# Attention weights turned through DRAM instead of by sixteen on-chip copies a head

## The chip, the cores and the metric

The kernel runs on one core of a Trainium2 chip. Its five engines (PE or TensorE, DVE or VectorE, ACT or ScalarE, POOL or GpSimd, SP or SyncE) have a queue each and run side by side; DMA engines move data between DRAM and SBUF. The metric is the device time of one execution in microseconds, the median of several runs.

## What is computed

One layer of an encoder: an RMS norm, one input projection, attention with eight query heads over two key/value heads and 512 tokens, a linear recurrence in both directions (LRU) over 1024 channels, a norm of each group by itself, gates, and one output projection.

```python
def hybrid_layer(x, ...):
    h = rms_norm(x, norm_w)
    proj = jnp.einsum('bsd,de->bse', h, w_in)          # 512 x 2048 by 2048 x 4608
    q, k, v, g_attn, xr, g_lru = jnp.split(proj, SPLITS, axis=-1)
    attn_out = attention_group(q, k, v, q_norm_w, k_norm_w)
    lru_out = lru_group(xr, conv_w, conv_b, lru_wa, lru_ba, lru_wx, lru_bx, lru_lambda)
    mixed = jnp.concatenate([rms_norm(attn_out, attn_norm_w) * jax.nn.silu(g_attn),
                             rms_norm(lru_out, lru_norm_w) * jax.nn.silu(g_lru)], axis=-1)
    return x + jnp.einsum('bse,ed->bsd', mixed, w_out)

def block(qb):                                         # in attention_group
    s = jnp.einsum('bkgqd,bksd->bkgqs', qb, k_t) * scale
    p = jax.nn.softmax(s, axis=-1)
    return jnp.einsum('bkgqs,bksd->bkgqd', p, v_t)
```

All is float32. Each product is made of three TensorE products of values split in a high and a low part (`mm3`: high by high, high by low, low by high).

## The kernel before

The work is one long program whose TensorE order is written out by hand. Generators are woven: `weave(fill, chain)` runs `chain`, and for each number n that it yields takes n steps of `fill`. The `fill` during attention is `gates()`, the projections for the gates: three groups of 512 columns (LRU gate in two halves, first half of the attention gate), each of 32 fill steps. A fill step is six matmuls of 128x128 by 128x512; four fill steps use up one chunk of `w_in`, 256 rows by 512 columns (512 KB). A chunk is loaded by SyncE (`wraw`, line 205) into a ring of three tiles, split by ACT (`wh`, line 216) and DVE (`wl`, line 217); during attention there are four pairs `wh`, `wl`, so room for two chunks. `take()` fetches the chunk two ahead of the one that it hands out.

`attention()` (line 644) is the `chain`. It first yields `BEGIN` = 8 fill steps, then goes through 32 steps, four (t = 0 to 3, one block of 128 queries each) for each of the eight heads, and six more for what lags. In a step `weights` makes one block of the attention weights: scores (`mm3` into a PSUM bank), row maximum (DVE), exponential (ACT, with the row sum), reciprocal (DVE), scaling (POOL, line 599) and a DVE transpose of 32x32 blocks into the tile `u` (line 600). `u` holds a head: on partition 32i + r, four sections a of 512 elements (2 KB). For the product with `v` the blocks must still change places between partitions: section a of partition group i has to go to partition group a, place i.

That is what `moved` does (line 605). Before, SyncE issues sixteen copies from SBUF to SBUF for each head, 32 partitions by 2 KB each (line 610): eight right after the head's last block, eight in the next step. Then ACT and DVE split the result `pt`, of which there is one buffer, into `ph` and `pl` (lines 620, 621). `values` (line 624), the product with `v`, comes `LATE` = 2 steps after the last block of the next head, that is six steps after the head's own last block: head h's `values` stand in step 4h + 9. It also adds the squares for the group norm (`asum`, line 642). Every step then yields `STEPS` = 2 fill steps.

During attention SyncE's order is written out too (`manual_schedule`): its DMAs leave in the order in which the program states them, and one that must wait holds all behind it. On SyncE are the loads of `w_in`, the copies for `moved`, and in steps 8 to 15 eight copies from DRAM to DRAM (`copy_to`, line 768). POOL issues 24 accumulating DMAs of 256 KB (`add_to`, line 771), one in each of steps 0 to 7 and 16 to 31, each behind the scaling of that step; their results are read only by the output product.

After attention twelve fill steps are left. Before, six of them are run, then the group statistics (`group_rstd`, line 685, eight small matmuls over `asum`), four more, `rows` (line 274, which spreads the result over the partitions), and the last two. Ahead of them in the program stand the builds of the four LRU pairs for the output product (`build`, `seven`: DVE and ACT). Then the fourth gate group (32 fill steps) is woven with `later()`, which normalizes two pairs of heads, yields 6, and gates them; then follows the output product (`outputs`, line 895 on TensorE).

Of the kernel before, what the change touches and what calls it, by code (L numbers as in the profile page):

```python
# [11 lines left out]
F32 = mybir.dt.float32  # L12
F32R = mybir.dt.float32r
# [4 lines left out]
P = 128  # L18
# [3 lines left out]
NT = SEQ // P  # L22
HD = 128
NH = 8
# [18 lines left out]
WARM, WARM2 = 14, 5  # L43


BEGIN, STEPS, LATE = 8, 2, 2


H = 256
# [2 lines left out]
B = 32  # L52
NQ = P // B
# [9 lines left out]
def hybrid_kernel(  # L63
# [20 lines left out]
    nc = tc.nc  # L84
# [28 lines left out]
    dram = ctx.enter_context(tc.tile_pool(name="dram", bufs=1, space=bass.MemoryType.DRAM))  # L113
# [3 lines left out]
    def nm(s):  # L117
        cnt[0] += 1
        return f"{s}_{cnt[0]}"
# [10 lines left out]
    def at(tag, bufs, shape, dt=F32):  # L130
        return pools["att"].tile([P, *shape], dt, tag=tag, bufs=bufs, name=nm(tag))
# [10 lines left out]
    def mm():  # L142
        return ps.tile([P, SEQ], F32, tag="mm", name=nm("mm"))

    def const(shape, name, dt=F32):
        return cp.tile(list(shape), dt, tag=name, name=name)

    def f(ap):
        return ap.bitcast(F32)
# [116 lines left out]
    def rsqrt_mean(dst, src, n, width):  # L266

        nc.gpsimd.tensor_scalar(dst, src, 1.0 / n, EPS, op0=ALU.mult, op1=ALU.add)
        nc.gpsimd.tensor_tensor(dst, dst, nhalf[:, :width], op=ALU.pow)
# [4 lines left out]
    def rows(dst, col, dg):  # L274

        shape = [P, NT, P]
        part = [const([P, NT], nm("part")) for _ in range(2)]
        parts = [dg() for _ in part]
        nc.vector.tensor_copy(part[0].bitcast(F32R), col)
        nc.vector.tensor_sub(part[1], col, part[0])  # L280
        for c, d in zip(part, parts):
            nc.vector.tensor_mul(
                d, ident[:, None, :].broadcast_to(shape), c[:, :, None].broadcast_to(shape)
            )
        pb = mm()
        for k, d in enumerate(parts):
            d = d.rearrange("p t q -> p (t q)")
            nc.tensor.matmul(pb, ones_r, d, start=k == 0, stop=k == 1)
        nc.vector.tensor_copy(dst, pb)
# [59 lines left out]
    def drain(fill):  # L349
        for _ in fill:  # L350
            pass
# [30 lines left out]
    sums = {}  # L382
# [197 lines left out]
    def turned(rot, h):  # L580

        q = at("q", 2, (2, SEQ), F32R)
        split_ps(turn(rot, h), q[:, 0, :], q[:, 1, :])
        return q[:, 0, :], q[:, 1, :]
# [3 lines left out]
    def weights(q, g, t, turned_):  # L588

        qh, ql = q  # L590
        tt = slice(t * P, (t + 1) * P)
        sc = mm()
        mm3(sc, qh[:, tt], ql[:, tt], kth[g], ktl[g], True, True)
        mx, sm = (at(n, 6, (1,)) for n in ("mx", "sm"))
        nc.vector.tensor_reduce(mx, sc, axis=AX.X, op=ALU.max, negate=True)  # L595
        p = at("p", 3, (SEQ,))
        nc.scalar.activation(p, sc, AF.Exp, bias=mx, accum_out=sm)  # L597
        nc.vector.reciprocal(sm, sm)  # L598
        last_scale[0] = nc.gpsimd.tensor_scalar(p, p, sm, 0.0, op0=ALU.mult, op1=ALU.add).ins  # L599
        nc.vector.transpose(  # L600
            turned_[:, :, :, t, :].rearrange("p a s c -> p s a c"),
            p.rearrange("p (s a c) -> p s a c", a=NQ, c=B),
        )

    def moved(turned_):

        pt = at("pt", 1, (NQ, NT, P))
        for i in range(NQ):
            for a in range(NQ):
                nc.sync.dma_start(  # L610
                    pt[a * B : (a + 1) * B, i].rearrange("p s x -> p (s x)"),
                    turned_[i * B : (i + 1) * B, a].rearrange("p s t c -> p (s t c)"),
                )
            if i % 2:
                yield
        hi, lo = at("ph", 1, (NT, SEQ), F32R), at("pl", 1, (NT, SEQ), F32R)
        hi4, lo4 = (v.rearrange("p s (i x) -> p i s x", i=NQ) for v in (hi, lo))
        for s in range(0, NT, 2):
            ss = slice(s, s + 2)
            nc.scalar.copy(hi4[:, :, ss], pt[:, :, ss])  # L620
            nc.vector.tensor_sub(lo4[:, :, ss], pt[:, :, ss], f(hi4[:, :, ss]))
        yield hi, lo

    def values(h, hi, lo):

        gs = slice(h // G * HD, (h // G + 1) * HD)
        o = mm()
        for s in range(NT):
            mm3(o, vh[s][:, gs], vl[s][:, gs], hi[:, s], lo[:, s], s == 0, s == NT - 1)
        if h % 2 == 0:  # L630
            ap_[h // 2] = aring.tile([P, 2, SEQ], F32, name=nm("av"))
        av, asum = ap_[h // 2][:, h % 2, :], sums["a"]
        nc.vector.tensor_copy(
            av.rearrange("p (t i c) -> p i t c", i=NQ, c=B),
            o.rearrange("p (i t c) -> p i t c", i=NQ, c=B),
        )
        if h == 0:
            nc.scalar.activation(asum, av, AF.Square)
        else:
            sq = at("p", 3, (SEQ,))  # L640
            nc.scalar.activation(sq, av, AF.Square)
            nc.gpsimd.tensor_add(asum, asum, sq)

    def attention(rots, transfers):

        qs, pts = {h: turned(rots[0], h) for h in range(1)}, {}
        yield BEGIN
        last = NH * NT
        for i in range(last + NT + LATE):
            h, t = divmod(i, NT)  # L650
            if i < last:
                if t == 0:
                    u = at("u", 2, (NQ, NT, NT, B))
                weights(qs[h], h // G, t, u)
                next(transfers, None)
                if t == 0 and h + 1 < NH:
                    qs[h + 1] = turned(rots[(h + 1) // G], (h + 1) % G)
                if t == NT - 1:
                    pts[h] = moved(u)
                    next(pts[h])  # L660
            if t == 0 and 0 < h <= NH:
                next(pts[h - 1])
                pts[h - 1] = next(pts[h - 1])
            h, t = divmod(i - LATE, NT)
            if t == NT - 1 and h > 0:
                values(h - 1, *pts.pop(h - 1))
            yield STEPS


    def gate(gs, pairs, row, sig):  # L670
# [11 lines left out]
    def fin_s(shape=(P, SEQ), dt=F32):  # L682
        return pools["fin"].tile(list(shape), dt, tag="s", bufs=2, name=nm("s"))

    def group_rstd(src, name, n):

        pr = mm()
        for t in range(NT):
            nc.tensor.matmul(
                pr[:, t : t + 1], src[:, t * P : (t + 1) * P], ones[:, 0:1], start=True, stop=True  # L690
            )
        r = const([P, NT], name)
        nc.vector.tensor_copy(r, pr[:, :NT])
        rsqrt_mean(r, r, n, NT)
        return r

    gbc = const([P, SEQ], "gbc")

    def normed(pair):
        nc.vector.tensor_mul(pair, pair, gbc[:, None, :].broadcast_to([P, 2, SEQ]))  # L700
# [27 lines left out]
    def kept(pool, i):  # L728
        return [
            pools[pool].tile([P, 7, H], F32R, tag=f"{t}{i}", bufs=1, name=nm(t))  # L730
            for t in ("mh", "ml")
        ]
# [302 lines left out]
    for step in proj_feat(C_XR, a1, first, given):  # L1035
# [8 lines left out]
        c, e = step  # L1044
# [17 lines left out]
    fill = proj_feat(C_XR + SEQ, a2)  # L1062
    wsums = first_sums()

    def with_sums(fill, n, first=0):

        for k, _ in enumerate(fill):
            if k >= first and (k - first) % n == 0:
                next(wsums, None)
            yield  # L1070

    fill = with_sums(fill, 8, 16)
# [23 lines left out]
    def both():  # L1096
        yield from q_proj(C_Q, a4)
        yield from q_proj(C_Q + SEQ, a5)

    fill = with_sums(both(), 5)  # L1100
# [40 lines left out]
    fill = gates()  # L1141
    with tc.manual_schedule(engines={mybir.EngineType.SP}):
        weave(fill, attention(rots, last_sums()))
# [14 lines left out]
    def build(i, pair, parts):  # L1158
        mixed[i][1] = parts
        seven(pair, *parts)  # L1160

    for q in range(4):
        build(q, hp[q], kept("fin", q))
    for _ in range(6):
        next(fill)
    with tc.high_priority():
        r = group_rstd(sums["a"], "r_a", NH * HD)
    for _ in range(4):
        next(fill)
    with tc.high_priority():  # L1170
        rows(gbc, r, lambda: fin_s((P, NT, P), F32R))
    drain(fill)


    def later():
        for pair in ap_[:2]:
            normed(pair)
        yield 6
        todo = gate(late, ap_[:2], R_AN, fin_s)
        for _ in range(3):  # L1180
            yield next(todo)
        build(4, ap_[0], [hring.tile([P, 7, H], F32R, name=nm(t)) for t in ("mh", "ml")])
        yield from todo
        for pair in ap_[2:]:
            normed(pair)

    acc = []
    fill = proj_feat(C_GA + SEQ, acc, take=take)
# [26 lines left out]
    last = ExitStack()  # L1215
# [47 lines left out]
```

## Time and profile before

| | us |
|---|---|
| median of three runs | 682.94 |
| the runs | 681.77 to 684.16 |
| the profiled execution | 681.03 |
| its span, first to last instruction | 679.3 |

The mean clock granted to TensorE over the span is 0.977 of full speed. In the page an engine's busy time counts its instructions without branches, semaphores and DMA issues; matmuls are pipelined, so PE's busy time isn't time at its peak. "PEld" is the loading of the stationary operand, "SPq" and the like an engine's queue, "DMA a<-b" a transfer from b to a. The chain that ended last is followed back from the last instruction, at each step to what released it. L610 is line 610 of the kernel. The lines themselves stand in the prediction, where they are used.

### The profile page before, as it was taken

The page shows a single profiled execution, that of the slowest core. Times are in us where ns is not written, and L with a number is a line of the kernel's source. Part 1 is how long each engine was busy: PE and PEld are TensorE (multiplying, and loading weights), DVE is VectorE, ACT ScalarE, POOL GpSimd, SP SyncE. Part 2 cuts the span into 40 slices and gives each one's busy share as a digit, 9 for nine tenths or more (in the row PEclk, how much of TensorE's full clock was granted, in tenths as well). Part 3 has the DMA queues.
Part 4 walks back from the last instruction along what each step waited for, and adds up shares of the span by engine and source line. Part 5 has one row for each costly group of instructions (what it writes and reads, how often), then busy time and mean ns, then how long its engine had stood idle before and what let it go on. Part 6 is the DMA issues. An engine that isn't in the chain of part 4 may idle for free.

```text
span 679.3 us, 8373 instructions
## 1 busy us (share of the span) xinstructions
PE 646.6 (95%) x2835; PEld 527.8 (78%) x2835; DVE 485.6 (71%) x788; ACT 346.2 (51%) x586; POOL 102.1 (15%) x137
## 2 busy tenths in 40 slices
PE   9999999999999998979879888799999999999997
PEld 7888888888888886867657766588888888888885
DVE  5888699958788638555855558438946777797775
ACT  3535997599468225433734337325524554444441
POOL 0001000100034003331113423202000000110010
PEclk9999999999999999998879989799999999999999
DMA  8854676666565312385366756752335675797252
GB/s 282 279 155 126 142 207 150 167 163 171 157 224 178 116 40 62 49 195 147 99 171 145 152 121 146 179 180 62 94 124 186 184 238 194 262 340 265 94 190 93
DMA packets 62459, 110.85 MB, mean 163 GB/s; under 512 B 6744, under 2 KB 17104, under 8 KB 62416
## 3 DMA queue, kind: packets, MB, share of 16 engines
q1 hardware_dynamic: 54384, 92.48, 42.0%
q0 software_dynamic: 7712, 17.31, 14.8%
q10 hardware_dynamic: 320, 0.53, 0.3%
q8 instruction: 22, 0.36, 0.2%
q14 instruction: 21, 0.17, 0.1%
HBM read 97.71 MB, written 25.17 MB: 181 GB/s over the span
## 4 chain that ended last, share of the span: by engine, by line
PE 79%; SPq 7%; DMA 5%; DVE 3%; ACT 3%; issue 2%; POOL 0%; DVEq 0%; ACTq 0%; POOLq 0%
PE pj L152 16%; PE pj L154 16%; PE pj L153 16%; PE mm L895 13%; PE pj L895 10%; SPq L610 6%; DMA wr<-in_w_in_dram 4%; PE mm L154 2%; PE mm L152 2%; PE mm L153 2%; DVE wl L217 1%; PE mm L242 1%; ACT wh L216 1%; PE pj L308 1%; DMA pt<-u 1%
## 5 line engine op out<-in xcount | busy, mean ns | idle before, releaser
L152 PE MATMUL pj<-x,wh 128*128 128x512 f32 x376 | 152.9, 407 | 20.6 <-ACT wh L216 20.6
L154 PE MATMUL pj<-x,wl 128*128 128x512 f32 x376 | 150.9, 401 | 2.9 <-DVE wl L217 2.9
L153 PE MATMUL pj<-x,wh 128*128 128x512 f32 x376 | 150.8, 401 | 0.0
L216 ACT CAST wh<-wr 128x512 fp32r<-128x512 f32 x143 | 83.9, 618 | 82.8 <-PE pj L154 26.1
L217 DVE TENSOR_TENSOR wl<-wr,wh 128x512 fp32r<-128x512 f32 x144 | 95.2, 694 | 33.5 <-ACT wh L216 25.3
L152 PEld LDWEIGHTS pj<-x,wh 128*128 128x128 f32 x376 | 73.1, 195 | 37.4 <-ACT wh L216 22.6
L747 ACT CAST wh<-wr 128x1024 fp32r<-128x1024 f32 (+1 forms) x72 | 60.6, 860 | 75.1 <-PE mm L895 37.8
L154 PEld LDWEIGHTS pj<-x,wl 128*128 128x128 f32 x376 | 72.8, 194 | 21.3 <-DVE wl L217 5.7
L748 DVE TENSOR_TENSOR wl<-wr,wh 128x1024 fp32r<-128x1024 f32 (+1 forms) x72 | 68.5, 983 | 25.5 <-ACT wh L747 25.4
L153 PEld LDWEIGHTS pj<-x,wh 128*128 128x128 f32 x376 | 73.3, 195 | 15.5 <-DVE x L245 0.3
L152 PE MATMUL pj<-wh,x 128*128 128x512 f32 x192 | 74.9, 390 | 0.0
L154 PE MATMUL pj<-wh,x 128*128 128x512 f32 x192 | 74.7, 389 | 0.0
L153 PE MATMUL pj<-wl,x 128*128 128x512 f32 x192 | 74.7, 389 | 0.0
L597 ACT ACTIVATE p<-mm,mx 128x512 f32<-128x512 f32 x32 | 22.1, 689 | 59.6 <-DVE mx L595 59.1
L895 PE MATMUL mm<-wl,mh 128*128 128x512 f32 x128 | 49.8, 389 | 0.0
L895 PE MATMUL mm<-wh,mh 128*128 128x512 f32 x128 | 49.8, 389 | 0.0
L895 PE MATMUL mm<-wh,ml 128*128 128x512 f32 x128 | 49.8, 389 | 0.0
L771 POOL DMA_DIRECT2D t<-in_w_out_dram x40 | 33.1, 837 | 101.9 <-DMA t<-in_w_out_dram 101.7
L154 PEld LDWEIGHTS pj<-wh,x 128*128 128x128 f32 x192 | 36.0, 188 | 7.6
L152 PEld LDWEIGHTS pj<-wh,x 128*128 128x128 f32 x192 | 36.0, 188 | 7.5
L153 PEld LDWEIGHTS pj<-wl,x 128*128 128x128 f32 x192 | 36.0, 188 | 7.4
L599 POOL TENSOR_SCALAR p<-p,sm 128x512 f32<-128x512 f32 x32 | 22.8, 712 | 118.4 <-DVE sm L598 103.0
(204 smaller groups left out, 1061.2 us busy)
## 6 DMA issues: line engine op xcount, KB each, us to landing
wr<-in_w_in_dram SPq DMA_DIRECT2D x71, 512.0 KB, 4.0
wr<-in_w_out_dram SPq DMA_DIRECT2D x24, 512.0 KB, 5.2
t<-in_w_out_dram POOLq DMA_DIRECT2D x40, 256.0 KB, 5.8
wr<-t SPq DMA_DIRECT2D x40, 256.0 KB, 4.2
pt<-u SPq DMA_DIRECT2D x128, 64.0 KB, 2.1
t<-in_w_out_dram SPq DMA_DIRECT2D x24, 256.0 KB, 5.5
t<-t SPq DMA_DIRECT2D x16, 256.0 KB, 4.2
wr<-in_w_out_dram SPq DMA_DIRECT2D x16, 256.0 KB, 5.2
```

The source lines that it names most:

```text
L152: nc.tensor.matmul(acc, lh, rh, start=start, stop=False)
L153: nc.tensor.matmul(acc, lh, rl, start=False, stop=False)
L154: nc.tensor.matmul(acc, ll, rh, start=False, stop=stop)
L216: copy(hi, raw[:, k, :])
L217: nc.vector.tensor_sub(lo, raw[:, k, :], f(hi))
L597: nc.scalar.activation(p, sc, AF.Exp, bias=mx, accum_out=sm)
L599: last_scale[0] = nc.gpsimd.tensor_scalar(p, p, sm, 0.0, op0=ALU.mult, op1=ALU.add).ins
L610: nc.sync.dma_start(pt[a * B : (a + 1) * B, i].rearrange("p s x -> p (s x)"), turned_[i * B : (i + 1) * B, a].rearrange("p s t c -> p (s t ...
L747: nc.scalar.copy(hi[:, to], b)
L748: nc.vector.tensor_sub(lo[:, to], b, f(hi[:, to]))
L771: nc.gpsimd.dma_start(dst, src, accum_op=ALU.add)
L895: nc.tensor.matmul(dst[s], lh[:, ts_], rh, start=i == 0 and j == 0, stop=i == 7 and j == 2)
```

## The change

`moved` writes the head's whole `u` (1 MB, 8 KB from each partition) to a tile in DRAM, one for each head, with one DMA, and reads it back with four DMAs of 256 KB, one for each partition group of `pt`, in runs of 2 KB (each run 8 KB from the next one). Both are issued by SyncE. The write stands in step t = 0 of the next head, the reads and the splits into `ph` and `pl` in its step t = 2. `LATE` becomes 3, so `values` of head h stand in step 4h + 10, seven steps after the head's last block, and attention has one step more. `BEGIN` becomes 10, and the first four steps after the last scores take three fill steps. Attention so uses 92 of the 96 fill steps instead of 84. The group statistics move into `later()`: two fill steps of the fourth gate group, the statistics, four steps, `rows` and the two pairs, and four steps instead of six before the gates.

```diff
-BEGIN, STEPS, LATE = 8, 2, 2
+BEGIN, STEPS, LATE = 10, 2, 3
...
     def moved(turned_):

+        aside_ = dram.tile([P, NQ, NT * P], F32, name=nm("pd"), tag="pd", bufs=NH)
+        nc.sync.dma_start(aside_, turned_.rearrange("p a s t c -> p a (s t c)"))
+        yield
         pt = at("pt", 1, (NQ, NT, P))
-        for i in range(NQ):
-            for a in range(NQ):
-                nc.sync.dma_start(
-                    pt[a * B : (a + 1) * B, i].rearrange("p s x -> p (s x)"),
-                    turned_[i * B : (i + 1) * B, a].rearrange("p s t c -> p (s t c)"),
-                )
-            if i % 2:
-                yield
+        src = aside_.rearrange("(i r) a x -> a r i x", r=B)
+        for a in range(NQ):
+            nc.sync.dma_start(
+                pt[a * B : (a + 1) * B].rearrange("p i s x -> p i (s x)"), src[a]
+            )
...
                 if t == NT - 1:
                     pts[h] = moved(u)
-                    next(pts[h])
             if t == 0 and 0 < h <= NH:
                 next(pts[h - 1])
+            if t == 2 and 0 < h <= NH:
                 pts[h - 1] = next(pts[h - 1])
...
-            yield STEPS
+            yield STEPS + (last <= i < last + NT)
...
-    for _ in range(6):
-        next(fill)
-    with tc.high_priority():
-        r = group_rstd(sums["a"], "r_a", NH * HD)
-    for _ in range(4):
-        next(fill)
-    with tc.high_priority():
-        rows(gbc, r, lambda: fin_s((P, NT, P), F32R))
     drain(fill)

     def later():
+        yield 2
+        with tc.high_priority():
+            r = group_rstd(sums["a"], "r_a", NH * HD)
+        yield 4
+        with tc.high_priority():
+            rows(gbc, r, lambda: fin_s((P, NT, P), F32R))
         for pair in ap_[:2]:
             normed(pair)
-        yield 6
+        yield 4
         todo = gate(late, ap_[:2], R_AN, fin_s)
```

## The prediction

> **What bounds the kernel now.** The page comes first: one core, its engines' busy time, and the chain that ended last.
>
> ```profile
> span 679.3 us, 8373 instructions
> PE 646.6 (95%) x2835; PEld 527.8 (78%) x2835; DVE 485.6 (71%) x788; ACT 346.2 (51%) x586; POOL 102.1 (15%) x137
> ...
> PE 79%; SPq 7%; DMA 5%; DVE 3%; ACT 3%; issue 2%; POOL 0%; DVEq 0%; ACTq 0%; POOLq 0%
> PE pj L152 16%; PE pj L154 16%; PE pj L153 16%; PE mm L895 13%; PE pj L895 10%; SPq L610 6%; DMA wr<-in_w_in_dram 4%; PE mm L154 2%; PE mm L152 2%; PE mm L153 2%; DVE wl L217 1%; PE mm L242 1%; ACT wh L216 1%; PE pj L308 1%; DMA pt<-u 1%
> ```
>
> TensorE is the bound, but 6% of the chain is SyncE's queue (SPq) on line 610, the line that the change takes out, and 4% is loads of `w_in`. Which stretch loses time, I read from the stages (columns: stretch, length, then busy time and count of PE, PEld, DVE, ACT, POOL, granted clock, DMA share, GB/s).
>
> ```profile
> 300.00:440.00 140.00, 116.54 (x463) 91.31 (x463) 86.93 (x142) 68.02 (x117) 37.26 (x47) 0.91 0.63 150
> 440.00:457.70 17.70, 17.70 (x76) 14.40 (x76) 5.64 (x7) 5.02 (x7) 1.30 (x1) 0.97 0.59 182
> 457.70:522.00 64.30, 64.30 (x289) 53.29 (x288) 47.39 (x71) 29.74 (x42) 3.43 (x3) 1.00 0.33 103
> ```
>
> All of it lies in attention: there PE idles 23.5 of 140 us and runs at clock 0.91; later it is full. PE's timeline shows the size of a stall, and that it is paid twice (brackets: idle before, and what ended it).
>
> ```profile
> 286.01 0.40 PE L152 MATMUL mm<-kt,q 128*128 128x512 f32 x1
> ...
> 296.83 0.40 PE L152 MATMUL mm<-kt,q 128*128 128x512 f32 x1
> ...
> 300.27 0.40 PE L152 MATMUL mm<-kt,q 128*128 128x512 f32 x1
> ...
> 300.98 0.60 PE L548 MATMUL mm<-ident,ev 128*128 128x128 f32 x4
> 305.44 0.79 PE L152 MATMUL pj<-x,wh 128*128 128x512 f32 x1 [3.86 <-ACT wh L216]
> ...
> 309.02 0.63 PE L154 MATMUL pj<-x,wl 128*128 128x512 f32 x1
> 309.45 0.63 PE L152 MATMUL pj<-x,wh 128*128 128x512 f32 x1
> ...
> 311.15 0.44 PE L153 MATMUL mm<-kt,q 128*128 128x512 f32 x1
> 311.43 0.39 PE L154 MATMUL mm<-kt,q 128*128 128x512 f32 x1
> ```
>
> A score matmul opens each step. A free step, three score matmuls and two fill steps of six, takes 300.27 - 296.83 = 3.44, so 0.229 a matmul. After the idle 3.86 they come 0.43 apart (309.02, 309.45) up to 311.2: thirteen of them, 0.2 too long each, 2.6 on top of the wait. The end of the last `values`:
>
> ```profile
> 457.48 0.39 PE L154 MATMUL mm<-ph,v 128*128 128x512 f32 x1
> ```
>
> From 300.27 (step 8) to 457.7 PE has, by the code, 58 fill steps (348 matmuls), 24 scores (72) and 8 `values` (96): 516 at 0.229 is 118.2, with five turns of four transposes (0.4 each) about 120. It took 157.4: **37 us lost**. The waits of PE in 300 to 440 name the cause (us in total, times, longest).
>
> ```profile
> PE pj L152 <- ACT wh L216: 20.6, 7, 4.9
> PE pj L154 <- DVE wl L217: 2.9, 4, 1.0
> ```
>
> So 23.5 is waiting for split weights and some 13.5 the slow matmuls behind the waits. Why the weights are late, SyncE's timeline shows, and the chain of waits behind the stall at 300.98.
>
> ```profile
> 246.08 18.96 SPq L205 DMA_DIRECT2D wr<-in_w_in_dram  x3
> ...
> 287.92 10.15 SPq L610 DMA_DIRECT2D pt<-u  x16
> 298.17 1.10 SPq L205 DMA_DIRECT2D wr<-in_w_in_dram  x2
> ```
> ```profile
> 287.20 0.70 DVE u L600
> ...
> 298.17 5.09 DMA wr<-in_w_in_dram
> ```
>
> SyncE keeps program order here. It stands from 265 to 287.9 for head 0's last transpose, then takes 10.15 us to issue sixteen copies, and two weight loads stand behind them. Their data lands 5.1 us later; PE wanted it at 301.
>
> **The change, part by part.**
>
> *Sixteen issues become five.* Per head 16 of 0.63 (10.15/16) go; one write and four reads come, 3.2 us if one costs as much (a 512 KB load took 1.10/2 = 0.55, so size doesn't show). By program order the write stands first; the next load is right behind, at T+0.6 instead of T+10.2, where T is when u is complete. That is 9.6 us earlier against a longest wait of 4.9. The four reads wait for the write to land, and the head's second load behind them. With the landing below (7) it goes out at about T+10, as now (298.7 = T+10.8), but isn't needed until 10 us later than the first. So both loads come in time, and the 37 us have no cause left at SyncE. What is late next is the transfer.
>
> *Cost of write and reads.* Landing times of the nearest issues (KB each, us):
>
> ```profile
> wr<-in_w_in_dram SPq DMA_DIRECT2D x71, 512.0 KB, 4.0
> ...
> wr<-t SPq DMA_DIRECT2D x40, 256.0 KB, 4.2
> pt<-u SPq DMA_DIRECT2D x128, 64.0 KB, 2.1
> ...
> wr<-in_w_out_dram SPq DMA_DIRECT2D x16, 256.0 KB, 5.2
> ```
> ```profile
> out_dram<-xt POOLq DMA_DIRECT2D x6, 256.0 KB, 3.8
> ...
> out_dram<-xt SPq DMA_DIRECT2D x2, 256.0 KB, 2.6
> ```
>
> A 1 MB write isn't in the trace. Below: 2.6, as if four times the bytes cost nothing; above: four times 3.8 = 15.2. I take 7, twice the POOL row, as nearest: 512 KB land in 4.0, no more than 256 KB. A read of 256 KB from rows 8 KB apart is most like the `in_w_out` row, 5.2; four follow 0.63 apart. Then the splits (mean ns after the busy time):
>
> ```profile
> L621 DVE TENSOR_TENSOR pl<-pt,ph 128x1024 fp32r<-128x1024 f32 x14 | 16.8, 1222 | 0.3 <-DMA wr<-in_w_in_dram 0.3
> L620 ACT CAST ph<-pt 128x1024 fp32r<-128x1024 f32 x14 | 14.0, 1045 | 0.2 <-PE pj L153 0.2
> ```
>
> T to split weights: 7 + 2.5 + 5.2 + two casts and one subtract 3.3 = 18 (bounds 13.6 and 26.2), against 10.2 + 2.1 + 3.3 = 15.6 now. The time there is, from the first score of the next head to `values` seven steps behind: six steps 20.6, two turns 0.8, the other head's `values` 2.7, three scores 0.7 = 24.8. T after that score was 287.9 - 286.0 = 1.9 in the calm first head, but where gates crowd DVE:
>
> ```profile
> 324.10 0.40 PE L152 MATMUL mm<-kt,q 128*128 128x512 f32 x1
> ```
> ```profile
> 330.65 0.70 DVE L600 STREAM_TRANSPOSE u<-p 128x512 f32<-128x512 f32 x1
> ```
>
> 331.35 - 324.10 = 7.2. Need 19.9 to 25.2, slack +4.9 to -0.4: it fits, barely, in the crowded heads.
>
> The Trainium skill, "DMA: Bandwidth & Descriptors", section "Anatomy of one DMA — SWDGE (gpsimd) path", fits one transfer by 2.0 us plus bytes over 436 GB/s, measured on the other queue kind; by it 1 MB would be an estimated 4.4 us, the chain about 15.5 and the slack never negative. The row of 512 KB at 4.0 (the fit: 3.2) says it is somewhat low here.
>
> *Twice the bytes.* Queues in 300 to 440 (packets, MB, share of 16 engines):
>
> ```profile
> q1 hardware_dynamic: 9945, 16.25, 37.6%
> q0 software_dynamic: 2557, 4.65, 24.8%
> ```
>
> 37.6% of 140 over 16.25 MB is 3.24 us a MB; the accumulating queue takes 34.7/4.65 = 7.5. A head in the new kernel: write, reads and two loads 3.15 MB, 10.2 us; four accumulations 1.05 MB, 7.8 (six heads; in two heads copies, 3.4). Sum 18.0, against 17.3 of PE a head without stalls (4 x 3.44, a turn, `values`). The DMA engines become about full in six heads: +0.7 each, 4 us. I add 6 for late `values` in crowded heads and their slow matmuls (two of 1 us with 2 of slow clock). If the accumulations yield instead, since nothing reads them before 500 us, it is nothing.
>
> *BEGIN 10.* Two more fill steps (2.7 us) cover the start of attention, where PE waits now:
>
> ```profile
> 268.86 0.50 PE L152 MATMUL mm<-kt,q 128*128 128x512 f32 x1 [1.93 <-ACT q L552]
> ...
> 270.77 0.79 PE L154 MATMUL mm<-kt,q 128*128 128x512 f32 x1 [1.19 <-DVE q L553]
> ```
>
> Up to 3.1 gone; the DVE chain there is the same, so I take 3, bounds 0 and 3.1.
>
> *LATE 3, the three-step yields, the statistics.* No work added. After the last `values` there were 46 fill steps to the output product and are now 2 + 4 + 32 = 38, 52 us where there were 64.3 (the third stage above). DVE's 47.4 us must fit: 91% instead of 74%. Cost 0 if it fits, and if not about the backlog, 47.4 - 0.8 x 52 = 6 us, 0.8 being the load it carries in attention without stalls (86.93 in some 105). I take 0, since the product begins with the LRU pairs, built first. The statistics run eight fills behind the last `values`, as before.
>
> **Sum.** -37 - 3 + 10 = -30 against the profiled 681.03 (span 679.3, 1.7 around it): 651. The runs' median, 682.94, lies 1.9 above the profiled one: **653**. All of the gain and none of the cost: 643.
>
> **Rivals.**
> (a) *The transfer takes SyncE's place.* If DMA at 18.0 us a head also slows what it carries, and in-order ACT stands at the casts of `pt` with the weight splits behind, each head waits some 2 us more, with slow matmuls 1 to 2: 3 to 4 a head, 8 heads, gain 5 to 22, 661 to 678. For: 97 to 105% of DMA. Against: the loads have some 10 us to spare, and a stall gives the DMA time back.
> (b) *Slower.* The write's landing as a wait at SyncE's head, and slow reads: from where T to split weights exceeds 23 us, PE waits for `values`, at once for two heads, since the next window contains the stall. To eat the 40 it takes four stalls of over 7.5 and 2.6 of slow clock each: T to split over 30, that is write and reads at twice my sum (14.7 to 27). At 35, four stalls of 12 + 2.6 = 58: 700. Against: no read here is that slow. For: no row of that size, beside accumulations.
> The Trainium skill states in the same section that a semaphore wait is served on the issuing sequencer before dispatch; SyncE standing from 265 to 287.9 agrees, and this rival is that rule with a landing over 20 us.
> (c) *No change.* The loads are late for the wait for u itself, not for the sixteen issues. The chain speaks against it: the issues stand between u and the load without a gap. Then 683.
>
> **Chances.** Forecast (gain 22 to 41) 0.60; (a) 0.25; (c) 0.05; (b) 0.10. The range from 642, all stalls gone, to 675 takes most of (a). This kernel's runs tell 0.3% (2 us) from no change: faster 0.85, within 0.3% 0.05, slower 0.10.
>
> **What would show it.** Right: line 610's sixteen rows gone; a weight load within 1 us of the write; PE's wait for `wh` in attention under 6 us; the stretch from step 8 to the last `values` near 130; clock over 0.97. Wrong: PE waiting at `mm<-ph,v`, ACT at `ph`, SyncE standing over 10 us before the reads, or a stall at the first output products.

## The result, and the profile after

The changed kernel takes 666.68 us in the median of four runs (666.52 to 667.53), the kernel before 683.42 on the same chip (681.77 to 684.16): a ratio of 0.976, 95% interval 0.974 to 0.978. The forecast was 653, the range 642 to 675. The gain is 16.7 us where 30 was forecast.

First the head of the page and its chain, to lay beside those of before.

```profile
span 664.8 us, 8258 instructions
PE 640.4 (96%) x2835; PEld 523.7 (79%) x2835; DVE 486.3 (73%) x788; ACT 346.6 (52%) x586; POOL 100.8 (15%) x137
...
PE 80%; DMA 5%; issue 5%; DVE 4%; POOL 3%; ACT 3%; SPq 0%; DVEq 0%; ACTq 0%; POOLq 0%
PE pj L152 16%; PE pj L153 16%; PE pj L154 16%; PE mm L895 11%; PE pj L895 9%; PE mm L153 3%; PE mm L154 3%; PE mm L152 3%; DMA wr<-in_w_in_dram 2%; DMA wr<-in_x_dram 1%; DVE pl L621 1%; POOL p L599 1%; PE mm L242 1%; DMA pd<-u 1%; PE pj L308 1%
```

SyncE's queue, 7% of the chain before, is gone from it, and so is line 610. The stages, with the columns as before (the second row is the stretch after attention):

```profile
300.00:445.00 145.00, 128.63 (x534) 101.60 (x533) 90.56 (x146) 72.30 (x124) 38.23 (x48) 0.95 0.84 213
445.00:507.00 62.00, 62.00 (x278) 51.34 (x277) 47.78 (x72) 28.99 (x41) 2.63 (x3) 1.00 0.35 108
```

PE still idles 16.4 us in attention at a clock of 0.95; the DMA engines' share has gone from 0.63 to 0.84. The waits of PE from 300 to 445 are two (us in total, times, longest):

```profile
PE mm L153 <- DVE pl L621: 10.0, 7, 2.0
PE mm L152 <- ACT ph L620: 6.3, 3, 2.6
```

No wait for `wh` or `wl` is left. PE waits for `ph` and `pl`, the split attention weights: `values` has become what is late. SyncE's timeline shows why the weights are in time.

```profile
302.18 0.35 SPq L608 DMA_DIRECT2D pd<-u  x1
302.62 1.48 SPq L768 DMA_DIRECT2D t<-t  x1
304.19 0.57 SPq L205 DMA_DIRECT2D wr<-in_w_in_dram  x1
...
312.00 1.74 SPq L613 DMA_DIRECT2D pt<-pd  x4
313.79 0.47 SPq L768 DMA_DIRECT2D t<-t  x1
314.31 0.59 SPq L205 DMA_DIRECT2D wr<-in_w_in_dram  x1
```

The write costs SyncE 0.35 us; the head's first load follows 2.0 us after it (within 0.5 in the six heads in which no copy from DRAM to DRAM stands between, 1.0 in head 2), the second behind the reads. But the reads of head 1 went out at 312.00, 9.8 us after the write. Landing times (KB each, us), and who held the reads (waits of SyncE from 262 to 460):

```profile
pd<-u SPq DMA_DIRECT2D x8, 1024.0 KB, 6.6
pt<-pd SPq DMA_DIRECT2D x32, 256.0 KB, 5.8
```
```profile
SPq L613 <- DMA pd<-u: 34.5, 7, 6.2
SPq L613 <- DVE pl L621: 29.1, 6, 7.6
```

The write landed in 6.6 and a read in 5.8, near the 7 and 5.2 of the sum. Yet the reads waited for `pl` about as long as for the write: there is one `pt`, and it is free only when the head before has been split. Why that is late, ACT's timeline shows in head 1.

```profile
322.28 0.58 ACT L552 CAST q<-mm 128x512 fp32r<-128x512 f32 x1
325.31 0.69 ACT L597 ACTIVATE p<-mm,mx 128x512 f32<-128x512 f32 x1 [2.45 <-DVE mx L595]
325.90 0.19 ACT L597 ACTIVATION_READ_ACCUMULATOR p<-mm,mx 128x1 f32 x1
328.50 0.69 ACT L597 ACTIVATE p<-mm,mx 128x512 f32<-128x512 f32 x1 [2.40 <-DVE mx L595]
329.08 0.19 ACT L597 ACTIVATION_READ_ACCUMULATOR p<-mm,mx 128x1 f32 x1
329.17 1.98 ACT L620 CAST ph<-pt 128x1024 fp32r<-128x1024 f32 x2
```

The last read of this head went out by 313.74 and no read takes over 7.7 us to land (the longest under this tile's name), so `pt` was complete by 321.5. ACT was idle twice after that, 2.45 and 2.40 us, and began the casts at 329.17. They stand in its queue behind the exponential of step 14, the step to which `values` of head 1 belongs (in head 2 it is so too; in heads 0, 3, 4 and 5 they stand one step ahead of that). In the last two heads no exponential stands between, and the casts do wait for the data, 1.7 and 2.3 us; PE waits for neither of these. In head 1 PE pays:

```profile
327.23 0.40 PE L154 MATMUL mm<-kt,q 128*128 128x512 f32 x1
330.26 0.50 PE L152 MATMUL mm<-ph,v 128*128 128x512 f32 x1 [2.63 <-ACT ph L620]
332.17 0.79 PE L153 MATMUL mm<-pl,v 128*128 128x512 f32 x1 [1.40 <-DVE pl L621]
332.76 0.63 PE L154 MATMUL mm<-ph,v 128*128 128x512 f32 x1
333.18 0.63 PE L152 MATMUL mm<-ph,v 128*128 128x512 f32 x1
```

PE does the scores of step 14, then has to wait until ACT has made that step's exponential, cast `ph`, and DVE has subtracted. After it the matmuls come 0.42 apart, at about half pace.

How much is lost is counted as in the prediction, from the first score of step 8 to the end of the last `values`:

```profile
299.54 0.40 PE L152 MATMUL mm<-kt,q 128*128 128x512 f32 x1
...
453.42 0.39 PE L154 MATMUL mm<-ph,v 128*128 128x512 f32 x1
```

The next matmul starts at 453.65. 552 matmuls (384 fill, 72 scores, 96 `values`) at 0.229 and five turns make 128.4; it took 154.1. So 25.7 us are lost in attention, against 37 before. These 11.3 and 2.4 at the first scores (3.1 us of waiting before, 0.7 now) make most of the 14.4 by which the profiled executions differ (681.03 and 666.61).

### The profile page after: what moved, and what is told of

It is laid out like the page before. It is cut to its first block, busy times and chain, and to the rows that moved or that the text cites. A ratio compares the mean times of both kernels' runs of the same rounds, so it can differ in the third digit from the quotient of the medians.

```text
span 664.8 us, 8258 instructions
## 1 busy us (share of the span) xinstructions
PE 640.4 (96%) x2835; PEld 523.7 (79%) x2835; DVE 486.3 (73%) x788; ACT 346.6 (52%) x586; POOL 100.8 (15%) x137
## 3 DMA queue, kind: packets, MB, share of 16 engines
q0 software_dynamic: 7712, 17.31, 14.4%
## 4 chain that ended last, share of the span: by engine, by line
PE 80%; DMA 5%; issue 5%; DVE 4%; POOL 3%; ACT 3%; SPq 0%; DVEq 0%; ACTq 0%; POOLq 0%
PE pj L152 16%; PE pj L153 16%; PE pj L154 16%; PE mm L895 11%; PE pj L895 9%; PE mm L153 3%; PE mm L154 3%; PE mm L152 3%; DMA wr<-in_w_in_dram 2%; DMA wr<-in_x_dram 1%; DVE pl L621 1%; POOL p L599 1%; PE mm L242 1%; DMA pd<-u 1%; PE pj L308 1%
## 5 line engine op out<-in xcount | busy, mean ns | idle before, releaser
L152 PE MATMUL pj<-x,wh 128*128 128x512 f32 x376 | 148.5, 395 | 0.0
L154 PE MATMUL pj<-x,wl 128*128 128x512 f32 x376 | 147.1, 391 | 0.0
L153 PE MATMUL pj<-x,wh 128*128 128x512 f32 x376 | 147.1, 391 | 0.0
L217 DVE TENSOR_TENSOR wl<-wr,wh 128x512 fp32r<-128x512 f32 x144 | 97.3, 708 | 30.1 <-ACT wh L216 30.0
L153 PEld LDWEIGHTS pj<-x,wh 128*128 128x128 f32 x376 | 70.9, 189 | 15.1 <-DVE x L245 0.3
L154 PEld LDWEIGHTS pj<-x,wl 128*128 128x128 f32 x376 | 70.8, 188 | 15.2
L152 PEld LDWEIGHTS pj<-x,wh 128*128 128x128 f32 x376 | 71.1, 189 | 14.8
L895 PE MATMUL pj<-wl,mh 128*128 128x512 f32 x96 | 37.5, 390 | 0.5 <-DVE wl L748 0.5
```

The costliest lines, as they stand in the source:

```text
L152: nc.tensor.matmul(acc, lh, rh, start=start, stop=False)
L153: nc.tensor.matmul(acc, lh, rl, start=False, stop=False)
L154: nc.tensor.matmul(acc, ll, rh, start=False, stop=stop)
L217: nc.vector.tensor_sub(lo, raw[:, k, :], f(hi))
L895: nc.tensor.matmul(dst[s], lh[:, ts_], rh, start=i == 0 and j == 0, stop=i == 7 and j == 2)
```

## The experiments

The theories: **Q**, the sixteen issues on SyncE made the loads late; **P**, the place of the transfer did, because a load stood behind something that waits. **O**, what is left is the order in ACT's and DVE's queues; **T**, `pt` comes too late, or **D**, the DMA engines are full. Eleven runs; ratios are to the kernel before on the same chip, with 95% intervals. Its median there was 683.42 for the change and 681.4 for each of the three groups e1 to e4, e5 to e9 and e10 to e12, so kernels of different groups, and all with the change, are better compared by ratio. The last columns are PE's waits in us in one execution, the profiled one, between 262 and 460, for weights (`wh`, `wl`) and for `ph`, `pl`.

| run | us | ratio | weights | `ph`, `pl` |
|---|---|---|---|---|
| before | 683.42 | 1 | 23.5 | 0 |
| the change | 666.68 | 0.976 (0.974 to 0.978) | 0 | 16.3 |
| e1_schedule_alone | 690.30 | 1.013 (1.010 to 1.016) | 27.5 | 0 |
| e2_transfer_alone | 682.29 | 1.001 (0.999 to 1.003) | 0 | 25.4 |
| e3_late4 | 663.14 | 0.973 (0.970 to 0.977) | 0 | 13.8 |
| e4_casts_first | 653.95 | 0.959 (0.957 to 0.961) | 0 | 10.1 |
| e5_splits_first | 649.52 | 0.953 (0.949 to 0.958) | 2.8 | 4.1 |
| e6_sixteen_reads | 670.57 | 0.985 (0.980 to 0.990) | 0.3 | 18.0 |
| e7_second_write | 663.92 | 0.973 (0.970 to 0.977) | 2.2 | 14.9 |
| e9_begin8 | 659.97 | 0.966 (0.962 to 0.971) | 1.0 | 9.4 |
| e10_copies_in_place | 654.20 | 0.960 (0.955 to 0.965) | 2.6 | 5.2 |
| e11_copies_splits_first | 651.03 | 0.955 (0.951 to 0.958) | 2.9 | 4.0 |
| e12_splits_first_again | 650.41 | 0.954 (0.950 to 0.958) | 1.6 | 5.3 |

### The two halves of the change, each alone

The schedule without the new transfer, on the kernel before:

```diff
-BEGIN, STEPS, LATE = 8, 2, 2
+BEGIN, STEPS, LATE = 10, 2, 3
...
-            yield STEPS
+            yield STEPS + (last <= i < last + NT)
```

and the statistics moved as in the change.

> Sixteen copies a head as before, with the changed kernel's BEGIN 10, LATE 3, three-step yields and moved statistics. Theory Q (the loads were late because sixteen issues stood ahead of them): the weight waits mostly stay, total of PE waiting for wh over 12 us, time 672 to 682. Rival S (moving fill steps against the copies is what helps, since a load now stands between the first eight and the second eight): waits for wh under 6 us, time 655 to 668, so that the way through DRAM brings nothing of its own.

It is slower than before, 690.3: Q's waits, but above its time. And the transfer without the schedule, from the changed kernel:

```diff
-BEGIN, STEPS, LATE = 10, 2, 3
+BEGIN, STEPS, LATE = 8, 2, 2
...
-            yield STEPS + (last <= i < last + NT)
+            yield STEPS
```

with the statistics where they were.

> The way through DRAM with BEGIN 8, LATE 2, two-step yields and the statistics where they were. Theory O (values wait because ACT's queue holds the casts of pt behind the exponential of the same step): in this kernel's queue the casts stand one exponential ahead of values' step in most heads, so no more waiting than in the changed kernel, 662 to 672. Rival T (pt lands too late, the DMA engines are full): one step less to land in costs up to 3.4 us in each of eight heads, 680 to 695.

682.3, no change. Neither half gains; only both together do. In e1 SyncE's timeline shows a load between the two groups of eight, and the copies held:

```profile
320.95 1.13 SPq L768 DMA_DIRECT2D t<-t  x2
331.96 4.95 SPq L610 DMA_DIRECT2D pt<-u  x8
336.96 1.17 SPq L205 DMA_DIRECT2D wr<-in_w_in_dram  x1
...
338.76 5.05 SPq L610 DMA_DIRECT2D pt<-u  x8
```
```profile
SPq L610 <- DVE pl L621: 55.1, 7, 10.5
```

The second fence is SyncE's longest wait there from 262 to 460: 55.1 us in which the copies stand for `pt` to be free, with loads behind them (30.6 in the kernel before). By the order in the program, the load behind the first eight is that of the chunk that PE takes in step 4h + 7, one step sooner than the one that stood behind the copies before (4h + 8). That this is why e1 is slower than the kernel before is argued from the order, not tried by itself.

In e2 I had expected 662 to 672 by O and the time lies in T's 680 to 695. The waits, though, are not T's in most heads. The two largest, 6.6 and 4.5 us, come from ACT's order in another form. In head 1 the last read went out by 313.92 and no read took over 8.1 us to land, so `pt` was complete by 322.0; ACT began the casts at 334.28:

```profile
329.34 1.28 ACT L676 ACT_TABLE_LOAD   x1
330.63 0.63 ACT L676 ACTIVATE ev<-ev 128x512 f32<-128x512 f32 x1
331.28 1.28 ACT L597 ACT_TABLE_LOAD   x1
332.57 0.69 ACT L597 ACTIVATE p<-mm,mx 128x512 f32<-128x512 f32 x1
...
334.28 1.99 ACT L620 CAST ph<-pt 128x1024 fp32r<-128x1024 f32 x2
```

Exponentials and gates (L676) alternate here, and each turn from one to the other costs a table load of 1.28, six of them between 319.99 and 332.56. Only the last head's casts stood for the data (7.9 us, `pt<-pd`). So e2 says that six steps are too few with ACT's queue as it is; only the last head shows the transfer as too slow.

### Is it time or order?

One step more for `values`:

```diff
-BEGIN, STEPS, LATE = 10, 2, 3
+BEGIN, STEPS, LATE = 10, 2, 4
```

> The changed kernel with LATE 4: values one step (3.45 us and two fill steps) later. Theories O and T both: the waits at values, 1.3 to 4.1 us a head, shrink or go with the slow clock behind them, 645 to 656. If the waits are not a latency but a throughput bound of the DMA engines (rival D), they come back at other places and it stays at 662 to 670.

663.1: the 3.4 us of each head bring 3.5 us in all at most (by ratio 0.973 against 0.976, with intervals that overlap). That is outside what O and T expected and inside D's 662 to 670, so e3 by itself leaves D open; e4, e5 and e11 bear on it below. The instruction order offers another reason. Exponentials ahead of the casts in ACT's queue, heads 0 to 5:

| kernel | exponentials ahead of the casts | scores ahead of `values` on PE |
|---|---|---|
| the change | 10, 15, 19, 22, 26, 30 | 11, 15, 19, 23, 27, 31 |
| e3_late4 | 10, 15, 20, 23, 27, 31 | 12, 16, 20, 24, 28, 32 |
| e4_casts_first | 9, 13, 17, 21, 25, 29 | 11, 15, 19, 23, 27, 31 |

With one step more in hand, the order in the queue moved back by one in four of the six heads too. So the casts were put first, and nothing else edited:

```diff
-        nc.scalar.activation(p, sc, AF.Exp, bias=mx, accum_out=sm)
+        with ExitStack() as behind:
+            if t == 1 and last_cast[0]:
+                behind.enter_context(tc.issue_after(last_cast[0]))
+            nc.scalar.activation(p, sc, AF.Exp, bias=mx, accum_out=sm)
...
-            nc.scalar.copy(hi4[:, :, ss], pt[:, :, ss])
+            last_cast[0] = nc.scalar.copy(hi4[:, :, ss], pt[:, :, ss]).ins
```

> The changed kernel, where in the second block of each head the exponential is held behind the casts of pt of the head two before, so that the casts leave ACT's queue at least one exponential earlier (nothing else is edited). Theory O: pt lay there 5 to 9 us before its casts began, so the waits at values fall below 5 us in all and the time is 645 to 655. Rival T: the casts now stand and wait for the reads, with the exponentials behind them, and the time is 663 to 675.

653.95, as O said, though the waits fell to 10 and not under 5 us. By the count of above attention loses 14.3 us where the change loses 25.7, and nearly all of the difference lies in heads 1 and 2, the two whose casts had stood behind the exponential of the very step: from the first score of step 14 to that of step 15 PE took 13.6 us in the change (326.76 to 340.40) and takes 8.2 in e4 (325.86 to 334.08), from step 18 to step 19 13.4 and 8.2. Head 1 now, in ACT's timeline and in PE's:

```profile
321.09 0.58 ACT L552 CAST q<-mm 128x512 fp32r<-128x512 f32 x1
321.56 2.02 ACT L623 CAST ph<-pt 128x1024 fp32r<-128x1024 f32 x2
324.12 0.69 ACT L600 ACTIVATE p<-mm,mx 128x512 f32<-128x512 f32 x1 [0.55 <-DVE mx L595]
```
```profile
326.56 0.40 PE L152 MATMUL mm<-ph,v 128*128 128x512 f32 x1
328.64 0.50 PE L153 MATMUL mm<-pl,v 128*128 128x512 f32 x1 [1.68 <-DVE pl L624]
328.98 0.39 PE L154 MATMUL mm<-ph,v 128*128 128x512 f32 x1
329.21 0.40 PE L152 MATMUL mm<-ph,v 128*128 128x512 f32 x1
```

The casts begin 7.6 us earlier (321.56 for 329.17) and don't wait for the data; `ph` is ready when PE comes. In three other heads the casts now do stand for the data, as T said, but 7.0 us in all, and PE waits for `ph` 0.3 us in all. What is left, 1.3 to 1.8 us in each of six heads, is `pl`: in DVE's queue the subtracts stand behind the row maximum of the same step.

```profile
326.76 0.69 DVE L595 TENSOR_REDUCE mx<-mm 128x1 f32<-128x512 f32 x1 [2.74 <-PE mm L154]
327.37 2.35 DVE L624 TENSOR_TENSOR pl<-pt,ph 128x1024 fp32r<-128x1024 f32 x2
```

DVE was idle 2.74 us before that maximum, with the casts done since 323.6. So the subtracts too were put first:

```diff
-        nc.vector.tensor_reduce(mx, sc, axis=AX.X, op=ALU.max, negate=True)
+        with ExitStack() as behind:
+            if t == 1 and last_sub[0]:
+                behind.enter_context(tc.issue_after(last_sub[0]))
+            nc.vector.tensor_reduce(mx, sc, axis=AX.X, op=ALU.max, negate=True)
...
-            nc.vector.tensor_sub(lo4[:, :, ss], pt[:, :, ss], f(hi4[:, :, ss]))
+            last_sub[0] = nc.vector.tensor_sub(lo4[:, :, ss], pt[:, :, ss], f(hi4[:, :, ss])).ins
```

> As e4, and DVE's row maximum in the second block of a head is held behind the subtracts of the same pt too. Theory O: in e4 six waits of 1.7 us at the second matmul of values were the subtracts standing behind the row maximum of that step; they go, with no slow clock behind them, so 12 us at most less than e4's 654: 641 to 646. Rival T: DVE now stands at the subtracts for pt, row maxima come later, 652 to 660.

649.5, the lowest median of all, 4.4 below e4; by ratio 0.953 against 0.959, with intervals that just meet, so that the size of this second step is not sure. It is 3.5 above what I expected: the six waits shrank to three, but PE now waits 2.8 us for weights as well (in the profiled execution, with 653.2 the slowest of the four).

### The place or the number of issues?

In the changed kernel, four reads are replaced by sixteen of 64 KB:

```diff
         for a in range(NQ):
-            nc.sync.dma_start(
-                pt[a * B : (a + 1) * B].rearrange("p i s x -> p i (s x)"), src[a]
-            )
+            for i in range(NQ):
+                nc.sync.dma_start(
+                    pt[a * B : (a + 1) * B, i].rearrange("p s x -> p (s x)"), src[a, :, i]
+                )
```

> The changed kernel with sixteen reads of 64 KB a head in place of four of 256 KB; the write and its place are as they were. Theory Q (the number of issues on SyncE is what made loads late): some 8 us more of issue a head before the second load and before the splits, waits for wh come back, 675 to 690. Rival P (what counts is that a load leaves ahead of the wait for pt): the first load of a head is still ahead and the second has about 10 us to spare, waits for wh stay under 3 us in all, 665 to 672.

Seventeen issues a head instead of five, and PE waits 0.3 us for weights: P, not Q. The time is 4 us above the changed kernel's, by ratio 0.985 against 0.976 with intervals that don't meet, though its runs spread over 668 to 674; where that comes from is not settled. Then the DRAM trip itself was taken out, and the sixteen copies from SBUF to SBUF put where the reads had been:

```diff
-        aside_ = dram.tile([P, NQ, NT * P], F32, name=nm("pd"), tag="pd", bufs=NH)
-        nc.sync.dma_start(aside_, turned_.rearrange("p a s t c -> p a (s t c)"))
         yield
         pt = at("pt", 1, (NQ, NT, P))
-        src = aside_.rearrange("(i r) a x -> a r i x", r=B)
-        for a in range(NQ):
-            nc.sync.dma_start(
-                pt[a * B : (a + 1) * B].rearrange("p i s x -> p i (s x)"), src[a]
-            )
+        for i in range(NQ):
+            for a in range(NQ):
+                nc.sync.dma_start(
+                    pt[a * B : (a + 1) * B, i].rearrange("p s x -> p (s x)"),
+                    turned_[i * B : (i + 1) * B, a].rearrange("p s t c -> p (s t c)"),
+                )
```

> The changed kernel without DRAM: the sixteen copies from SBUF to SBUF of before, but all in step t = 2 of the next head, where the changed kernel has its reads. Rival P (the place of the transfer against the loads is what helps): waits for wh stay under 5 us in all and the time is 658 to 672, near the changed kernel's 667. Theory Q (sixteen issues make the loads late wherever they stand) or a need for DRAM: waits for wh over 12 us, 675 to 692.

654.2: it beats the changed kernel by 12 (0.960 against 0.976) without the DRAM trip, and beats the expectation. SyncE's timeline:

```profile
341.87 10.04 SPq L611 DMA_DIRECT2D pt<-u  x16
351.95 1.12 SPq L205 DMA_DIRECT2D wr<-in_w_in_dram  x2
```

The picture is that of before, sixteen copies in ten microseconds and two loads behind them; but the first load behind them is another one. By the order in the program it is fetched in step 4h + 7 and PE takes its chunk in step 4h + 11; before, the load behind the copies was that of the chunk for step 4h + 8. The load for step 4h + 9 leaves ahead of the copies, as it does ahead of the reads in the change. That part of the lead over the changed kernel is the order again is argued from the queue: here the casts stand behind 8, 12, 17, 22, 26 and 30 exponentials, earlier in three heads and at the same place in three. With casts and subtracts first in both, the two ways of transfer were compared on one chip.

> e10 with the casts and subtracts of pt first, as in e5. If the place and the order are all that counts: 643 to 652, as e5, with 8 MB less moved in each direction. If the copies' ten microseconds of issue on SyncE are late for something here: waits for wh, over 655.

> The kernel of e5 on the chip of e10 and e11, to compare e11 with it: 646 to 653.

651.0 (650.7 to 651.2) and 650.4 (649.8 to 652.0): no difference, though e11, the first, moves 1 MB a head less in and out of DRAM. Once the place and the order are right, the way through DRAM gains and costs nothing to within about 1 us.

### Are the DMA engines full?

e4 with a second write of the same megabyte a head to a place that nothing reads:

```diff
+        again = dram.tile([P, NQ, NT * P], F32, name=nm("pe"), tag="pe", bufs=NH)
+        nc.sync.dma_start(again, turned_.rearrange("p a s t c -> p a (s t c)"))
```

> As e4 with one more write of the same 1 MB a head to a place in DRAM that nothing reads. Theory O (order, with the DMA engines not the limit): the reads come up to 3.5 us later, which e4's waits partly cover, 654 to 664. Rival D (the DMA engines are full, 0.83 of them busy in attention): 8 MB more at 3.2 us a MB is 27 us of their time, of which attention has some 18 left, 666 to 685 with waits for wh.

663.9, at the upper end of O's expectation and 10 above e4. It is inconclusive as to D: PE's largest wait, 4.6 us in head 0, is ACT's order once more, this time with the casts behind two gates, so the edit moved the queue too. What speaks against D as the cause of the change's loss is e5: there the DMA engines are busier than in the change, and attention runs faster (first row the change, second e5).

```profile
300.00:425.00 125.00, 108.63 (x446) 85.14 (x445) 81.60 (x135) 63.94 (x112) 35.48 (x45) 0.95 0.82 205
```
```profile
300.00:425.00 125.00, 120.87 (x523) 97.14 (x523) 94.24 (x144) 71.93 (x122) 38.42 (x48) 0.99 0.91 231
```

At a share of 0.91 PE idles 4 us of 125, and at 0.82 it idles 16. That e11, with 1 MB a head less each way, is no faster than e12 says the same.

### BEGIN

e4 with BEGIN 8:

```diff
-BEGIN, STEPS, LATE = 10, 2, 3
+BEGIN, STEPS, LATE = 8, 2, 3
```

> As e4 with BEGIN 8. The two fill steps ahead of attention then no longer cover the first query's transposes: waits of about 2 and 1 us at the first scores come back, 655 to 659. If the place of a load against the write matters more (with BEGIN 8 the chunk is taken in even steps, so the head's second load stands ahead of the reads' step differently), waits for wh show and it is over 662.

660.0, 6 more than e4, a microsecond above what was expected. The waits of 1.9 and 1.2 us at the first scores are back; the runs spread (655.8 to 660.3) and what makes the other 3 us isn't settled.

## Why the prediction was right or wrong

**In the range, and partly by luck.** 667 lies in 642 to 675, but the forecast's own outcome, a gain of 22 to 41, did not come: the gain is 16.7. The range holds it because it takes in most of rival (a)'s band, and the cause is not (a)'s. Of the signs, the rows of line 610 and the waits for `wh` went, as they should; the stretch from step 8 to the last `values` took 154, not near 130, PE waits at `mm<-ph,v` (16.3 us with `pl`), and SyncE stood over 10 us before the reads in heads 3 and 5 (11.8 and 10.4). The clock, 0.988, says little, since it was over 0.97 before.

**Right: the bound, and what the change takes away.** The 37 us lost in attention were waits for weights and the slow matmuls behind them; those waits fell from 23.5 us to none, the first load leaves within 2 us of the write, in six heads within 0.5, and the second has time behind the reads. The landing times were sized well (6.6 for 7, 5.8 for 5.2), and the statistics cost nothing: PE is full from 445 to 507.

**Right in size: BEGIN.** 3 was taken. PE's wait at the first scores fell from 3.1 to 0.7.

**Wrong: the chain from u to the split weights.** The step "T to split weights: 7 + 2.5 + 5.2 + two casts and one subtract 3.3 = 18" adds the casts as if they began when the data lands. In head 1 they began some 7.7 us after it (321.5 to 329.2), because their place in ACT's queue is behind the exponential of the very step in which `values` stands; from u complete (302.2) to the end of the casts (331.2) it took 29. The prediction asked what slows the data and never where the consumer stands in its engine's queue. Rival (a) had ACT standing at the casts for data; in heads 0 to 5 the trace shows the reverse, data waiting for the casts, in head 1 while ACT idles (in the last two heads the casts stood 4.0 us in all for data, which cost PE nothing). The late splits also held `pt`, and with it the reads (29.1 us), which the sum didn't have.

**Mis-sized: the cost of 10.** It was 4 for full DMA engines and 6 for late `values`; by the count of the prediction 25.7 us stay lost. e4 and e5 show that some 12 and then 16 us of the total are the queue order alone (13 and 17 by the medians, 12 and 16 by the ratios). The 4 for the DMA engines was not seen: e5 has them busy for 0.91 of attention and is the fastest kernel. The step to that 4 also holds a slip: 4 x 3.44, a turn of 0.4 and `values` of 2.7 make 16.9 of PE a head and not 17.3, so that by its own argument the term was nearer 7.

**Wrong in its reason: "sixteen issues become five".** The issues on the chain were real, but e6 and e10 show that sixteen of them don't make the loads late (0.3 and 2.6 us of waiting for weights), if the load behind them is one that PE takes late. e1 is the other side: with the same sixteen in the old place and the new schedule, the loads stay late. The prediction's SyncE timeline, with the queue standing from 265 to 287.9, held the answer: what counts is which load stands behind the wait and the issues together, and when PE takes its chunk.

**Rivals.** (b), slower, didn't come, since neither write nor read was near twice its estimate; (c), no change, is what e2 gives, by another mechanism. The time lies in (a)'s band of 661 to 678, from another cause; (a)'s own 3 to 4 us a head would take 24 to 32 of the 40, a gain of 8 to 16, so its band was wider than its sum.

## What to carry to other kernels

When a producer is moved, look up where the consumer stands in the order of its own engine: here a wait "for ACT" while ACT was idle just before meant that the instruction stood behind another one that wasn't ready, and one edge of order was worth 12 us, where another way of transfer was worth nothing. On a queue in program order, count what is behind each instruction that waits; copies that took ten microseconds to issue did no harm here, once they stood behind the load that PE needs next. And try the parts of a change singly: here each half gained nothing, and the part that looked like the point, the way through DRAM, could be left out.

## What the runs showed of the hardware

A wait of 1.7 us by itself didn't slow the matmuls after it, and two waits close together can: in e4's rows above the matmuls after 1.68 idle come 0.23 apart (granted clock over the span 0.997), in the change those after 2.63 and 1.40, with one matmul between, come 0.42 apart. The same pair of waits can do both: at the first scores, after 1.93 and 1.19 with two matmuls between, the next come 0.43 apart in the kernel before (272.64 and 273.07), and after 1.94 and 1.19 they come 0.23 apart in e9 (272.00 and 272.23). The Trainium skill, "TensorE: Matmul & The Clock Gate", section "Part 1: The HAM clock gate (the "warmup" mystery)", puts the fall to the slow clock behind at least one idle window of about 3.4 us; the change's two waits sum to 4.0 and neither reaches it alone, so the page holds here only for the sum, and the 3.1 of the kernel before don't reach it even as a sum.

SyncE's issue time didn't grow with the bytes: in the change the 1 MB write took 0.34 to 0.35 us and four reads of 256 KB mostly 1.74, that is 0.44 each; in the kernel before a copy of 64 KB between SBUF partitions took 0.63.
